# Three edits of a two-layer encoder trunk: last norm's sum, index transposes, last heads of mixer one

## The chip, the cores and the metric

The kernel runs on one core of a Trainium2 chip. The metric is device time in microseconds (us) of one execution, lower is better, as the median of three runs. Beside the timed runs one execution was profiled; its trace is what the rows below are read from. PE is TensorE (matrix multiplies, which write to PSUM), PEld its weight loads, DVE VectorE, ACT ScalarE, POOL GpSimd, SP the engine whose queue issues the loads and stores.

## What is computed

The reference runs 512 tokens of width 1024 through two layers and a last norm, in float32. Cut to what matters here:

```
h = x
layer 0: h = h + even_mixer(rms_norm(h));  h = h + ffn(rms_norm(h))
layer 1: h = h + odd_mixer(rms_norm(h));   h = h + ffn(rms_norm(h))
out = rms_norm(h)            # h * rsqrt(mean(h*h) + 1e-6) * gain

even_mixer, heads A: score[t,s] = sum over 4 index heads of w[t,h] * relu(q_idx[t,h] . k_idx[s])
                     each token keeps its 128 best keys, then softmax attention on those
            heads B: softmax attention with a bias by distance
```

Each mixer half has eight heads; they are worked off in four pairs.

## The kernel before, in words

The residual `h` is held with channels on the partitions: eight blocks of 128 channels by 512 tokens. Each product is made of three matmuls on operands that are split into a high and a low part (`mm3`, lines 179 to 181). Weights come in tiles of 512 KB through SP's queue in the fixed order of a plan and are split by ACT (line 140) and DVE (line 141). A helper `hilo` (lines 186 and 187) splits activations the same way.

The program is written as generators that give out matmuls one unit at a time, so that work on DVE, ACT and POOL lies beside them. `Later` (lines 157 to 172) holds functions that come due after a count of ticks; a tick is given when a token tile of a projection is complete or a channel block is. The order in which an engine gets its instructions isn't the order of the text: when the program is built, a planner puts each engine's instructions in an order by priority (text order) and by when it reckons their inputs to be ready, and after that every engine works strictly in that order. `keep_in_program_order` pins an instruction behind everything already written for its engine.

**The index branch** (lines 641 to 710). Four token tiles of 128 tokens are projected; `evac_idx` norms and rotates one into a tile `qr`, and pushes `turn`, which transposes three 128x128 pieces of it on PE (line 662), splits them with `hilo`, and so fills `iq` and `ik`. All four were pushed with a count of 2. Then the value projection of heads B runs in four pieces (lines 713 to 721): the first completes token tile 0, the second tile 1, the third tile 2, the fourth tile 3, each with a tick. After the second, third and fourth piece the index scores of block 1, 2 and 3 are computed (`idx_scores`, matmuls on line 690); block i needs token tiles 0 to i. Each is followed by its top-k on DVE (`topk`, 16 rounds of two instructions), which runs a round at a time beside later work. `qr` has two buffers, so the third token tile's `qr` can be written only after the first one's transposes.

**The attention pairs** (class `Pair`). `weave(prev, cur, ...)` mixes the transposes and value products of one pair with the scores and softmax of the next. For head e of a pair `soft` adds the bias and takes the minimum on DVE (line 479), the exponential and its sum on ACT (line 481); `norm` takes the reciprocal of four sums on DVE (line 486, pinned) and multiplies four tiles on POOL (line 489); `turn` transposes on PE (line 499); `av` multiplies with the values (lines 516 and 517); `store` ends the head. `norm(0)` stood after the next transposes of the pair before, `norm(1)` at the very end of a `weave`, behind the `store` of the pair before.

**The last norm** (lines 883 to 910). The squares of the first seven channel blocks are summed into `hold_ss` on POOL as the blocks of the last feed-forward product come. The eighth block is computed in two halves of 256 tokens. In the middle of each half `lead_sums` (line 888) adds up `hold_ss` over the partitions: a matmul per token tile with the squares stationary and one column of ones moving, so the sum of a token lands on the partition of that token. When a half is done, `finish` squares the new block on ACT (line 900), adds its sums the same way (line 902), takes root and reciprocal over two columns (lines 197 and 198), and calls `roots` (lines 245 to 254): a diagonal matrix of the roots on DVE (line 248) and a matmul with ones (line 251) bring each token's root to all partitions. Four products (line 909) and four stores (line 910) end the half. fp32 matmuls of this kind are shown as two records each.

Of the kernel before, what the change touches and what calls it, by code (L numbers as in the profile page):

```python
# [10 lines left out]
F32 = mybir.dt.float32  # L11
F32R = mybir.dt.float32r
AF = mybir.ActivationFunctionType
# [4 lines left out]
SEQ = 512  # L18
NT = SEQ // 128
# [67 lines left out]
def trunk(ctx, tc, a, out):  # L87
    nc = tc.nc
# [115 lines left out]
    hold_ss = {}  # L204
# [226 lines left out]
    class Pair:  # L431
# [42 lines left out]
        def soft(self, e, rows):  # L474
            at = {1: 3, 2: 0, 0: 1, 3: 2}
            nms, sms = self.nm[e], self.sm[e]
            for i in rows:
                L, nm, sm = self.L[e][i], nms[:, at[i]:at[i] + 1], sms[:, at[i]:at[i] + 1]
                nc.vector.tensor_tensor_reduce(out=L, in0=self.s[e][i], in1=self.job["bias"][e][i], scale=1.0,
                                               scalar=3e38, op0=OP.add, op1=OP.min, accum_out=nm)  # L480
                nc.scalar.activation(L, L, AF.Exp, scale=-1.0, bias=nm, accum_out=sm)

        def norm(self, e):
            at = {1: 3, 2: 0, 0: 1, 3: 2}
            sms = self.sm[e]
            tc.keep_in_program_order(nc.vector.reciprocal(sms, sms))
            for i in (1, 2, 0, 3):
                L = self.L[e][i]
                nc.gpsimd.tensor_scalar(L, L, sms[:, at[i]:at[i] + 1], 1.0, op0=OP.mult, op1=OP.mult)
# [140 lines left out]
    with ExitStack() as st:  # L630
# [10 lines left out]
        def evac_idx(t, o):  # L641
            raw = mp.tile([128, 5, HD], F32, name="ir", tag="Y", bufs=2)
            nc.scalar.activation(raw.rearrange("p a d -> p (a d)"), o[:, 0:320], AF.Copy, scale=rs[:, t:t + 1])
            nc.vector.tensor_scalar(wi[:, t, :], o[:, 320:324], rs[:, t:t + 1], None, op0=OP.mult)
            st6 = smp.tile([128, 6], F32, name="st6", tag="s6")
            mv = smp.tile([128, 2], F32, name="mv", tag="s2")
            nc.vector.bn_stats(st6, raw[:, 4])
            nc.vector.bn_aggr(mv, st6)
            rstd = smp.tile([128, 1], F32, name="rstd", tag="s1")
            inv_root(rstd, mv[:, 1:2])  # L650
            kk = raw[:, 4]
            nc.vector.tensor_scalar(kk, kk, mv[:, 0:1], rstd, op0=OP.subtract, op1=OP.mult)
            nc.vector.tensor_tensor(kk, kk, lng[:, 0], OP.mult)
            nc.vector.tensor_tensor(kk, kk, lng[:, 1], OP.add)
            qr = sp.tile([128, 6, HD], F32, name="scr2", tag="scr2", bufs=2)
            rope(raw, t, 1, qr[:, 0:5], 5, mp.tile([128, 1024], F32, name="P", tag="P", bufs=2))
            nc.gpsimd.tensor_copy(qr[:, 5], qr[:, 4])

            def turn():
                pt = bank("tp", (128, 4, 128))  # L660
                for b in range(3):
                    nc.tensor.transpose(pt[:, b, :], qr[:, 2 * b:2 * b + 2].rearrange("p a d -> p (a d)"), ident)
                ts_ = slice(t * 128, (t + 1) * 128)
                hilo(iq[:, 0, :, ts_], iq[:, 1, :, ts_], pt[:, 0:2])
                hilo(ik[:, 0, 0, ts_], ik[:, 1, 0, ts_], pt[:, 2])
            later.push(2, turn)

        def at(k):
            pass
# [44 lines left out]
        for f in tok_group("vB", 512, evac_v(VB, 8)):  # L714
            run(f)
            vb += 1
            if vb >= 2 and vb < 5:
                if vb == 2:
                    later.drain()
                idx_scores(vb - 1)  # L720
                aside.q.append(topk(vb - 1))

# [68 lines left out]
        for p in range(4):  # L791
            if p == 2:
                later.drain()
            job = dict(qk=qkA[p], pair=pairs[4 + p], V=lambda e, p=p: VA["t"][:, :, 2 * p + e],
                       bias=[[cmask, work[1], work[2], work[3]]] * 2)
            cur = Pair(mp, job, 2)
            weave(pend, cur, fill, FILL_A[p])
            if p == 0:
# [84 lines left out]
    sums = {}  # L883

    def lead_sums(cols):
        pt = sums["t"] = bank("tp", (128, NT))
        for t in range(cols.start // 128, cols.stop // 128):
            nc.tensor.matmul(pt[:, t:t + 1], hold_ss["t"][:, t * 128:(t + 1) * 128], ones[:, 0:1],
                             start=t * 128 == cols.start, stop=False)

    def finish(c, cols):
        if c < KD - 1:
# [1 line left out]
            nc.scalar.activation(H["h"][:, c, :], H["h"][:, c, :], AF.Copy, scale=gT[:, 4, c:c + 1])  # L894
            return
        w = cols.stop - cols.start
        t0, t1 = cols.start // 128, cols.stop // 128
        pt = sums["t"]
        sq = sp.tile([128, SEQ], F32, name="os", tag="os", bufs=1)
        nc.scalar.activation(sq[:, cols], H["h"][:, c, cols], AF.Square, scale=1.0 / 32.0)  # L900
        for t in range(t0, t1):
            nc.tensor.matmul(pt[:, t:t + 1], sq[:, t * 128:(t + 1) * 128], ones[:, 0:1], start=False,
                             stop=t == t1 - 1)
        nc.scalar.activation(H["h"][:, c, cols], H["h"][:, c, cols], AF.Copy, scale=gT[:, 4, c:c + 1])
        inv_root(rs[:, t0:t1], pt[:, t0:t1])
        r = roots(t0, t1, False)[:, :w]
        for c0, c1 in ((0, 1), (1, 3), (3, 5), (5, 8)):
            v = H["h"][:, c0:c1, cols]
            nc.vector.tensor_tensor(v, v, r[:, None, :].to_broadcast([128, c1 - c0, w]), OP.mult)
# [383 lines left out]
```

## Time and profile before

| | us |
|---|---|
| median of three runs (1224.76 to 1226.49) | 1225.92 |
| the profiled execution | 1225.8 |
| its span, first to last instruction | 1223.8 |
| PE busy in the span | 1204.8 |
| DVE busy | 807.2 |
| ACT busy | 590.6 |
| POOL busy | 192.9 |

Times in the trace count from the start of the span. "Idle before" in square brackets is how long the engine had no instruction running before this one, and what ended that. A row of a timeline merges instructions of one kind that follow one another on their engine (x4), so its length can hold gaps. A matmul's length holds its way through the array: matmuls start closer together than they are long.

### The profile page before, as it was taken

Reading aid. Unit: us, or ns where it says so; the run is one execution under the profiler, and the core shown is the slowest. Engines: PE = TensorE matmul, PEld = TensorE weight load, DVE = VectorE, ACT = ScalarE, POOL = GpSimd, SP = SyncE. Lnnn points to the kernel's source line nnn. Section 1 sums busy time; section 2 is a strip of 40 time slices with the busy share of each in tenths; the row PEclk is TensorE's granted clock in tenths of the full one; section 3 lists DMA queues with packets and bytes.
Section 4 is the critical chain, followed back from the end, with each engine's and each line's share of the span. In section 5 each row is a group of like instructions: output and inputs, shape, how many; then the busy total and the mean of one; then the engine's idle time right before and its main releaser. Section 6 shows DMA issues by size and latency. Waiting matters only on the chain.

```text
span 1223.8 us, 15865 instructions
## 1 busy us (share of the span) xinstructions
PE 1204.8 (98%) x5918; PEld 993.6 (81%) x5918; DVE 807.2 (66%) x1424; ACT 590.6 (48%) x1001; POOL 192.9 (16%) x273
## 2 busy tenths in 40 slices
PE   9999999999999999999999999999999999999997
PEld 8788778877888888888888877778888888888886
DVE  7988987868777777743325466887777777762222
ACT  6555565655444444423224577775544444442221
POOL 1365313131000000000111254322000000000000
PEclk9999999999999999999999999999999999999998
DMA  8232223213332332333322311212332232322311
GB/s 270 69 104 70 87 63 121 70 35 121 104 103 88 102 98 92 104 100 99 95 68 81 121 53 37 70 52 70 104 104 88 102 101 89 104 92 98 103 52 69
DMA packets 35517, 111.70 MB, mean 91 GB/s; under 512 B 4209, under 2 KB 6897, under 8 KB 35441
## 3 DMA queue, kind: packets, MB, share of 16 engines
q1 hardware_dynamic: 35296, 110.68, 28.7%
q8 instruction: 46, 0.75, 0.3%
q14 instruction: 31, 0.25, 0.1%
q10 hardware_dynamic: 144, 0.02, 0.0%
HBM read 108.59 MB, written 2.10 MB: 90 GB/s over the span
## 4 chain that ended last, share of the span: by engine, by line
PE 82%; DVE 9%; ACT 3%; issue 3%; POOL 1%; DMA 1%; SPq 0%; DVEq 0%; POOLq 0%; ACTq 0%
PE acc L179 18%; PE acc L180 18%; PE acc L181 18%; PE s L179 8%; PE s L180 8%; PE s L181 8%; DVE wlo L141 2%; PE tp L499 1%; DVE wk L707 1%; PE tp L516 1%; DVE m L706 1%; PE tp L517 1%; PE s L458 1%; DVE PTl L187 1%; DVE xT L233 1%
## 5 line engine op out<-in xcount | busy, mean ns | idle before, releaser
L141 DVE TENSOR_TENSOR wlo<-raw,whi 128x1024 fp32r<-128x1024 f32 (+3 forms) x189 | 231.8, 1228 | 152.1 <-ACT whi L140 149.2
L140 ACT ACTIVATE whi<-raw 128x1024 fp32r<-128x1024 f32 (+3 forms) x197 | 204.7, 1039 | 218.9 <-PE acc L180 150.8
L179 PE MATMUL acc<-xT,whi 128*128 128x512 f32 x480 | 189.7, 395 | 0.2 <-DVE scr L598 0.2
L180 PE MATMUL acc<-xT,whi 128*128 128x512 f32 x480 | 187.0, 390 | 0.5 <-DVE xT L233 0.5
L181 PE MATMUL acc<-xT,wlo 128*128 128x512 f32 x480 | 187.1, 390 | 0.0
L216 POOL TENSOR_TENSOR scr<-scr,os 128x512 f32<-128x512 f32 x24 | 33.7, 1406 | 709.6 <-ACT os L214 709.6
L179 PE MATMUL acc<-act,whi 128*128 128x512 f32 (+1 forms) x374 | 141.1, 377 | 0.0
L180 PE MATMUL acc<-act,whi 128*128 128x512 f32 (+1 forms) x374 | 141.0, 377 | 0.0
L181 PE MATMUL acc<-act,wlo 128*128 128x512 f32 (+1 forms) x374 | 140.8, 376 | 0.0
L179 PE MATMUL s<-xT,whi 128*128 128x512 f32 x352 | 136.9, 389 | 0.0
L181 PE MATMUL s<-xT,wlo 128*128 128x512 f32 x352 | 136.9, 389 | 0.0
L180 PE MATMUL s<-xT,whi 128*128 128x512 f32 x352 | 136.9, 389 | 0.0
L179 PEld LDWEIGHTS acc<-xT,whi 128*128 128x128 f32 x480 | 90.2, 188 | 20.0 <-issue 1.5
L181 PEld LDWEIGHTS acc<-xT,wlo 128*128 128x128 f32 x480 | 90.1, 188 | 19.3 <-DVE wlo L141 0.2
L180 PEld LDWEIGHTS acc<-xT,whi 128*128 128x128 f32 x480 | 90.2, 188 | 18.9 <-DVE xT L233 0.9
L179 PE MATMUL acc<-whi,xT 128*128 128x512 f32 (+2 forms) x208 | 85.3, 411 | 0.4 <-DVE VB L191 0.2
L181 PE MATMUL acc<-whi,xT 128*128 128x512 f32 (+2 forms) x208 | 81.3, 391 | 0.2 <-DVE xT L233 0.2
L180 PE MATMUL acc<-wlo,xT 128*128 128x512 f32 (+2 forms) x208 | 81.5, 392 | 0.0
L186 ACT ACTIVATE act<-scr 128x512 fp32r<-128x512 f32 x44 | 27.7, 631 | 110.2 <-DVE scr L854 110.2
L181 PEld LDWEIGHTS acc<-act,wlo 128*128 128x128 f32 x374 | 70.4, 188 | 13.0
L180 PEld LDWEIGHTS acc<-act,whi 128*128 128x128 f32 x374 | 70.4, 188 | 12.9
L179 PEld LDWEIGHTS acc<-act,whi 128*128 128x128 f32 x374 | 70.4, 188 | 12.8
(246 smaller groups left out, 2168.4 us busy)
## 6 DMA issues: line engine op xcount, KB each, us to landing
raw<-in_w SPq DMA_DIRECT2D x188, 512.0 KB, 3.4
h<-in_x SPq DMA_DIRECT2D x16, 256.0 KB, 5.4
T<-in_relb SPq DMA_DIRECT2D x8, 256.0 KB, 2.6
raw<-in_w_d SPq DMA_DIRECT2D x4, 264.0 KB, 2.8
out_y<-h SPq DMA_DIRECT2D x4, 256.0 KB, 2.2
raw<-in_w_i SPq DMA_DIRECT2D x3, 324.0 KB, 5.1
out_y<-h SPq DMA_DIRECT2D x2, 384.0 KB, 2.4
ropeC<-in_ropeC SPq DMA_DIRECT2D x2, 256.0 KB, 4.4
```

Source lines behind the costliest of these rows:

```text
L140: nc.scalar.activation(hi[:, x], raw[:, x], AF.Copy)
L141: eng.tensor_tensor(lo[:, x], raw[:, x], hi[:, x].bitcast(F32), OP.subtract)
L179: nc.tensor.matmul(o, lh, rh, start=start, stop=False)
L180: nc.tensor.matmul(o, lh, rl, start=False, stop=False)
L181: nc.tensor.matmul(o, ll, rh, start=False, stop=stop)
L186: nc.scalar.activation(dh, src, AF.Copy)
L187: nc.vector.tensor_tensor(dl, src, dh.bitcast(F32), OP.subtract)
L216: eng.tensor_tensor(ss, ss, sq, OP.add)
L233: nc.vector.scalar_tensor_tensor(xT[1][:, c, :], H["h"][:, c, :], g, xT[0][:, c, :].bitcast(F32), op0=OP.mult, op1=OP.subtract)
L458: ins = nc.tensor.matmul(self.s[e][i], qk[r, b, 0, i * 128:w], qk[r, c, 1, 0:w], start=n == 0, stop=n == 2)
L499: nc.tensor.transpose(pt[:, off:off + 128], self.L[e][i][:, j * 128:(j + 1) * 128], ident)
L516: nc.tensor.matmul(o[:, j * 128:512], v, th[:, off:off + w], start=j == 0, stop=False)
```

## The change

It does three things. The last norm's sums are taken by a matmul with the 128x128 square of ones stationary and the squares moving, which puts each token's sum on every partition; root and reciprocal then run over 128x256, into `R`, and `roots` is no longer called there. The index transposes come due two token tiles at a time: tiles 0 and 1 after two ticks, tiles 2 and 3 after three, and the drain before the first scores goes. For the last pair of the first mixer `norm` is called at the end of `soft`, without the pin, and the later calls return at once.

```diff
--- before.py
+++ after.py
@@ -479,11 +479,17 @@
                 nc.vector.tensor_tensor_reduce(out=L, in0=self.s[e][i], in1=self.job["bias"][e][i], scale=1.0,
                                                scalar=3e38, op0=OP.add, op1=OP.min, accum_out=nm)
                 nc.scalar.activation(L, L, AF.Exp, scale=-1.0, bias=nm, accum_out=sm)
-
-        def norm(self, e):
+            if self.job.get("soon") and len(rows) > 1:
+                self.norm(e, False)
+
+        def norm(self, e, later=True):
+            if later and self.job.get("soon"):
+                return
             at = {1: 3, 2: 0, 0: 1, 3: 2}
             sms = self.sm[e]
-            tc.keep_in_program_order(nc.vector.reciprocal(sms, sms))
+            ins = nc.vector.reciprocal(sms, sms)
+            if later:
+                tc.keep_in_program_order(ins)
             for i in (1, 2, 0, 3):
                 L = self.L[e][i]
                 nc.gpsimd.tensor_scalar(L, L, sms[:, at[i]:at[i] + 1], 1.0, op0=OP.mult, op1=OP.mult)
@@ -663,7 +669,7 @@
                 ts_ = slice(t * 128, (t + 1) * 128)
                 hilo(iq[:, 0, :, ts_], iq[:, 1, :, ts_], pt[:, 0:2])
                 hilo(ik[:, 0, 0, ts_], ik[:, 1, 0, ts_], pt[:, 2])
-            later.push(2, turn)
+            later.push(2 + t // 2, turn)
 
         def at(k):
             pass
@@ -715,8 +721,6 @@
             run(f)
             vb += 1
             if vb >= 2 and vb < 5:
-                if vb == 2:
-                    later.drain()
                 idx_scores(vb - 1)
                 aside.q.append(topk(vb - 1))
 
@@ -792,7 +796,7 @@
             if p == 2:
                 later.drain()
             job = dict(qk=qkA[p], pair=pairs[4 + p], V=lambda e, p=p: VA["t"][:, :, 2 * p + e],
-                       bias=[[cmask, work[1], work[2], work[3]]] * 2)
+                       bias=[[cmask, work[1], work[2], work[3]]] * 2, soon=p == 3)
             cur = Pair(mp, job, 2)
             weave(pend, cur, fill, FILL_A[p])
             if p == 0:
@@ -883,10 +887,9 @@
     sums = {}
 
     def lead_sums(cols):
-        pt = sums["t"] = bank("tp", (128, NT))
-        for t in range(cols.start // 128, cols.stop // 128):
-            nc.tensor.matmul(pt[:, t:t + 1], hold_ss["t"][:, t * 128:(t + 1) * 128], ones[:, 0:1],
-                             start=t * 128 == cols.start, stop=False)
+        w = cols.stop - cols.start
+        sums["t"] = bank("tp")[:, :w]
+        nc.tensor.matmul(sums["t"], ones, hold_ss["t"][:, cols], start=True, stop=False)
 
     def finish(c, cols):
         if c < KD - 1:
@@ -894,16 +897,12 @@
             nc.scalar.activation(H["h"][:, c, :], H["h"][:, c, :], AF.Copy, scale=gT[:, 4, c:c + 1])
             return
         w = cols.stop - cols.start
-        t0, t1 = cols.start // 128, cols.stop // 128
-        pt = sums["t"]
-        sq = sp.tile([128, SEQ], F32, name="os", tag="os", bufs=1)
-        nc.scalar.activation(sq[:, cols], H["h"][:, c, cols], AF.Square, scale=1.0 / 32.0)
-        for t in range(t0, t1):
-            nc.tensor.matmul(pt[:, t:t + 1], sq[:, t * 128:(t + 1) * 128], ones[:, 0:1], start=False,
-                             stop=t == t1 - 1)
+        sq = sp.tile([128, SEQ], F32, name="os", tag="os", bufs=1)[:, :w]
+        nc.scalar.activation(sq, H["h"][:, c, cols], AF.Square, scale=1.0 / 32.0)
+        nc.tensor.matmul(sums["t"], ones, sq, start=False, stop=True)
         nc.scalar.activation(H["h"][:, c, cols], H["h"][:, c, cols], AF.Copy, scale=gT[:, 4, c:c + 1])
-        inv_root(rs[:, t0:t1], pt[:, t0:t1])
-        r = roots(t0, t1, False)[:, :w]
+        r = R[:, cols]
+        inv_root(r, sums["t"])
         for c0, c1 in ((0, 1), (1, 3), (3, 5), (5, 8)):
             v = H["h"][:, c0:c1, cols]
             nc.vector.tensor_tensor(v, v, r[:, None, :].to_broadcast([128, c1 - c0, w]), OP.mult)
```

## Rows read from the trace of the kernel before

**Rows 1.** The page, parts 1 and 4: TensorE's busy time, and the chain by engine.

```profile
PE 1204.8 (98%) x5918; PEld 993.6 (81%) x5918; DVE 807.2 (66%) x1424; ACT 590.6 (48%) x1001; POOL 192.9 (16%) x273
...
PE 82%; DVE 9%; ACT 3%; issue 3%; POOL 1%; DMA 1%; SPq 0%; DVEq 0%; POOLq 0%; ACTq 0%
```

**Rows 2.** Timeline, all engines, after the last matmul; columns: start us, us, instruction, idle before.

```profile
1214.41 0.42 DVE L384 TENSOR_TENSOR h<-acc,h 128x256 f32<-128x256 f32 x1 [2.15 <-PE acc L181]
...
1215.34 0.60 PE L902 MATMUL tp<-ones,os 128*128 128x1 f32 x4 [0.96 <-ACT os L900]
...
1217.03 0.87 PE L251 MATMUL tp<-os,ones 128*128 128x256 f32 x2 [1.08 <-DVE os L248]
...
1217.94 2.48 DVE L909 TENSOR_TENSOR h<-h,tp 128x256 f32<-128x256 f32 x4 [0.96 <-PE tp L251]
```

**Rows 3.** Timeline, PE, the first half's broadcast between the second half's matmuls.

```profile
1209.15 0.59 PE L251 MATMUL tp<-os,ones 128*128 128x256 f32 x2
```

**Rows 4.** Busy time by stretches of 4 us; granted clock (PEclk) third from the end.

```profile
1212.00:1216.00 4.00, 2.98 (x24) 2.69 (x23) 0.69 (x2) 0.94 (x3) 0.00 (x0) 1.00 0.59 208
...
1216.00:1220.00 4.00, 0.87 (x2) 0.30 (x2) 2.65 (x6) 0.25 (x1) 0.00 (x0) 0.68 0.12 42
```

**Rows 5.** Groups by line and shape, ACT; after the bar: busy us, mean ns.

```profile
L1007 ACT ACTIVATE G<-s,nF 128x256 f32<-128x256 f32 x8 | 3.7, 477 | 0.1
```

**Rows 6.** The same view, DVE.

```profile
L384 DVE TENSOR_TENSOR h<-acc,h 128x256 f32<-128x256 f32 x2 | 0.8, 425 | 9.8 <-PE acc L181 9.8
...
L198 DVE RECIPROCAL rs<-rs 128x4 f32<-128x4 f32 x4 | 0.7, 174 | 1.1 <-ACT rs L197 1.1
...
L198 DVE RECIPROCAL rstd<-rstd 128x1 f32<-128x1 f32 x4 | 0.6, 154 | 0.1
...
L198 DVE RECIPROCAL rs<-rs 128x2 f32<-128x2 f32 x2 | 0.3, 166 | 4.1 <-ACT rs L197 4.1
```

**Rows 7.** Chain of waits, last 29 us: start us, us, what.

```profile
1196.14 0.23 PE acc L180
...
1200.54 0.34 PE tp L888 x4
...
1206.02 0.56 PE tp L902 x4
...
1209.32 0.43 PE tp L251 x2
```

**Rows 8.** Timeline around the index transposes: PE, POOL, DVE.

```profile
34.03 0.82 PE L662 MATMUL tp<-ident,scr 128*128 128x128 f32 x6
...
38.40 0.85 PE L662 MATMUL tp<-ident,scr 128*128 128x128 f32 x6 [0.73 <-POOL scr L657]
...
39.18 0.97 PE L690 MATMUL s<-qk 64*128 64x256 f32 x12
...
38.10 0.23 POOL L657 COPY scr<-scr 128x64 f32<-128x64 f32 x1
...
37.20 1.38 DVE L187 TENSOR_TENSOR qk<-tp,qk 128x256 fp32r<-128x256 f32 x4
```

**Rows 9.** Timeline around the last heads of the first mixer: ACT, POOL, PE.

```profile
243.73 0.19 ACT L481 ACTIVATION_READ_ACCUMULATOR P<-P,nm 128x1 f32 x1
...
246.08 2.06 POOL L489 TENSOR_SCALAR P<-P,sm 128x256 f32<-128x256 f32 x4 [12.35 <-DVE sm L486]
...
250.20 2.07 POOL L489 TENSOR_SCALAR P<-P,sm 128x256 f32<-128x256 f32 x4 [2.06 <-DVE sm L486]
...
247.53 1.32 PE L499 MATMUL tp<-ident,P 128*128 128x128 f32 x8 [0.76 <-POOL P L489]
...
281.71 0.50 PE L180 MATMUL acc<-xT,whi 128*128 128x512 f32 x1 [0.47 <-DVE xT L233]
```

**Rows 10.** Timeline, PE, two earlier waits of the first mixer.

```profile
144.86 0.66 PE L499 MATMUL tp<-ident,P 128*128 128x128 f32 x4 [1.59 <-DVE nm L479]
...
170.35 0.39 PE L458 MATMUL tp<-qk 64*128 64x256 f32 x1 [1.31 <-DVE PTl L187]
```

## The prediction

> **What bounds the kernel now.** I read the page first: TensorE is busy for 98% of the span, and the chain that ended last runs for 82% of its length through TensorE's matmuls [rows 1]. So an edit can change the time in three ways only: it adds or removes matmul time, it opens or closes a stretch in which TensorE waits, or it changes the tail behind the last matmul. The second reading was therefore the timeline of the tail; the third was TensorE's own timeline around the index transposes and around the last heads of the first mixer, with what ended its waits. The stages between these places, the two feed-forward blocks above all, are not edited.
>
> The profiled execution took 1225.8 us, 0.1 below the median of the three runs (1225.92); its span is 1223.8, so 2.0 lie around the span. The sum below is made against 1225.8.
>
> **Part 1, the final sum: the tail.** What followed the last matmul is in [rows 2]: the column sums (L902, starting at 1215.34), a root and a reciprocal over two columns, the diagonal (L248), its broadcast by a matmul with ones (L251, 0.87), and at 1217.94 the first product (L909). From L902's start to L909's that is 2.60 us. The new path has three steps: a matmul with the square of ones stationary and 256 columns moving, which leaves the sum on every partition; a root over 128x256; a reciprocal over 128x256. The diagonal and its broadcast go.
>
> - The matmul. Its form, fp32 with 256 moving columns in two passes, is L251's. That took 0.59 in the first half [rows 3] and 0.87 in the tail, where TensorE had just waited for 1.08 [rows 2] and the granted clock of the 4 us was 0.68, after 1.00 in the 4 us before [rows 4]. The new one stands where L902 stands, in the stretch still at 1.00: 0.59, upper end 0.87.
> - The root. The nearest row is an activation with a bias pointer out of PSUM over 128x256: 0.48 [rows 5]. I take it.
> - The reciprocal. No row has it wide. With 1 element per partition it took a mean of 154 ns, with 2 166, with 4 174 [rows 6]: 20 ns for three further elements, 6.7 each. The other bound is an ordinary two-operand instruction over 128x256, 0.43 us [rows 6]. At 6.7 ns, 255 further elements make 0.15 + 1.71 = 1.86 us. I take that, because rows of the operation itself are nearer than a row of another. Ends: 0.43, and 3.2 by the 12 ns between 1 and 2 elements.
>
> With 0.15 for the hand-overs (three gaps of some 0.05, as between L251's end at 1217.90 and L909's start at 1217.94 [rows 2]): 0.59 + 0.48 + 1.86 + 0.15 = 3.08 in place of 2.60, **+0.48**. With the low end it is 1.65, **-0.95**.
>
> [...]
>
> **Part 1, on TensorE before the tail.** In the first half the sums and the broadcast stand between matmuls: 0.34 for L888, 0.56 for L902, which holds a wait of some 0.15, and 0.43 for L251 [rows 7]: 1.33. They become two matmuls of L251's kind, 0.43 each, with the same wait: 1.01, **-0.32**. In the second half L888's 0.34 becomes 0.43, **+0.09**. The wide reciprocal of the first half costs nothing: it lengthens VectorE's work on that half by less than its own 1.86 us, as the diagonal goes, and VectorE had idled 2.15 before the second half's residual add at 1214.41 [rows 2]. Without that cover it would cost up to 1.86. The first half's stores leave SP's queue up to 1 us earlier or later, long before the last ones are queued behind them. Part 1 together: **+0.25**.
>
> **Part 2, index transposes.** In the old order all four token tiles come due together. TensorE runs the transposes of tiles 0 and 1 at 34.03, then matmuls of the projection, waits 0.73 us on GpSimd's copy for tile 3 (it ends at 38.33), runs the other six, and only then the first index scores [rows 8]. The change puts tiles 2 and 3 one piece of the value projection later; the drain that goes found its queue empty before, and would otherwise undo the move. What is late next is the first scores' own input: VectorE finishes splitting tiles 0 and 1 at 37.20 + 1.38 = 38.58 [rows 8], and those matmuls are over at 38.40 - 0.73 = 37.67. If the scores stay there, they wait 1.0 (0.9 and a hand-over) in place of the 0.73; if more matmuls are put ahead of them, they wait for nothing. Later the scores of block 2 wait for tile 2's split. The splits of the first pair ended 4.55 us after its transposes began, 3.7 after they ended [rows 8]; the 12 matmuls of the last piece can cover 12 x 0.23 = 2.7 of that [rows 7]. The number of transposes, splits and scores is unchanged, and no DMA moves. Ends: -0.73, and +4.0 (rival 3). I take half of the gain, **-0.4**: of the two placements one takes the wait away and the other leaves it.
>
> **Part 3, last heads.** The normalising moves up behind the exponentials. For head 0 of the last pair the sums were complete at 243.73 + 0.19 = 243.92, and GpSimd's four products ran only from 250.20 to 252.27 [rows 9], so some 6 us of lateness go. But TensorE did not wait for them. Its waits near here are 0.76 for the pair before, whose normalising stays where it was (products from 246.08), and 0.47 at 281.71 for VectorE's split of the normed input [rows 9]. Only the second can shrink, if the heads end earlier and VectorE starts its residual work sooner. Against that, GpSimd may now take the last pair's head 0 ahead of the pair before: its four products take 2.07, from about 244.2 to 246.3 if they start as the sums come, which makes the pair before 0.2 late; if they start just ahead of 246.08, it is 2.07 late. Ends -0.47 and +2.07; near the first, as GpSimd idled 12.35 us up to 246.08. I take **-0.1**.
>
> **Sum:** +0.25 - 0.4 - 0.1 = -0.25, so 1225.8 - 0.25 = **1225.5 us**.
>
> **Rivals.**
> 1. *The wide reciprocal is cheap* (0.43). Then part 1 is -0.95 - 0.32 + 0.09 = -1.18 and the sum -1.7: 1224.1 us. For it: an ordinary 128x256 instruction takes that. Against: three further elements took 20 ns, where an ordinary instruction's 425 ns over 256 elements make 5 for three.
> 2. *The waits go as meant.* Both marked waits (-0.73 and -0.47) and part of the first mixer's waits on VectorE, 1.59 at 144.86 and 1.31 at 170.35 [rows 10], whose place hangs on when the index work comes in: with half of those two, 1.45, and the dear reciprocal's +0.25 that is -2.4, with the cheap one -3.8: 1223.4 to 1222.0 us. For it: each of these waits stands in the trace. Against: the edits take no work off VectorE.
> 3. *Slower: the second scores wait behind their own transposes.* If the planner puts the scores of block 2 right behind the transposes of tiles 2 and 3, the 3.7 us stand bare on TensorE, with everything queued behind them. With 1.0 for the first scores in place of 0.73 that is +4.0, and with parts 1 and 3 the sum is +4.2: 1230.0 us. Each matmul between takes 0.23 off: with up to 6 there the kernel is slower by more than can be taken for no change (below), with all 12 of the last piece the sum is +1.4. For it: VectorE runs the first top-k rounds just then. Against: the last piece and the next projection are ready.
> 4. *The heads' part does nothing:* TensorE's order stays, and the sum is -0.15: 1225.6, inside the forecast.
>
> **How the numbers follow.** About 0.2%, 2.45 us, is what a measurement of this kernel can tell from no change; against the median the bounds are 1223.5 and 1228.4. Forecast with rival 4: 0.46, all within. Rival 1: 0.20, within but for 0.04. Rival 2: 0.20, beyond the bound but for 0.02. Rival 3: 0.14, slower but for 0.02, when some of the matmuls cover. Faster 0.22, same 0.66, slower 0.12. The range is 1222.4 to 1228.0. Downward it takes in rival 1 and most of rival 2; upward the reciprocal at its upper end (+1.3) with the pair before late by half its bound (+1.0); it leaves out rival 3 and rival 2's edge.
>
> **What would show it.** Right: a reciprocal over 128x256 near 1.9 us in both halves, no diagonal and no broadcast matmul, the first product 3.1 us after the last column sum begins; the first index scores ahead of the transposes of tiles 2 and 3; the last pair's products on GpSimd near 244, with TensorE's waits there as before. Wrong: a reciprocal under 0.6 or over 2.4, a wait above 1 us at the second index scores, or waits of the first mixer that change outside these places.

## The result, and the profile after

The changed kernel takes 1232.84 us, the median of six runs (1230.63 to 1235.56); the kernel before, beside it, 1225.8 (six runs). The ratio is 1.0062 [1.0052, 1.0072]: **slower**, by 0.5 to 0.7%. Predicted were 1225.5 (1222.4 to 1228.0) and a chance of 0.12 for slower. The profiled execution took 1231.66, its span is 1229.6: 5.8 us more than before. The six runs lie in two groups, 1230.63 to 1231.66 us at a mean granted clock of 0.996 to 0.997 and 1234.02 to 1235.56 at 0.992 to 0.993, and the median lies in the gap between them.

TensorE's busy time is nearly the same, 1205.3 us against 1204.8, with 12 matmul records fewer. The page's parts 1 and 4, to set beside [rows 1]:

```profile
PE 1205.3 (98%) x5906; PEld 993.1 (81%) x5906; DVE 811.1 (66%) x1422; ACT 591.3 (48%) x1001; POOL 194.8 (16%) x273
...
PE 86%; DVE 8%; ACT 3%; issue 1%; POOL 1%; DMA 0%; SPq 0%; DVEq 0%; ACTq 0%; POOLq 0%
```

**The tail** went as predicted. Its timeline (TensorE, ScalarE, VectorE), to set beside [rows 2]:

```profile
1220.71 0.70 PE L902 MATMUL tp<-os,ones 128*128 128x256 f32 x2 [0.96 <-ACT os L901]
1221.45 0.47 ACT L197 ACTIVATE R<-tp,epsc 128x256 f32<-128x256 f32 x1 [0.25 <-PE tp L902]
1221.95 1.75 DVE L198 RECIPROCAL R<-R 128x256 f32<-128x256 f32 x1 [1.75 <-ACT R L197]
1223.74 2.50 DVE L908 TENSOR_TENSOR h<-h,R 128x256 f32<-128x256 f32 x4
```

From the column sum's start to the first product it is 3.03 us (2.60 before), and the wide reciprocal takes 1.75.

**The index scores** did not. TensorE's timeline, to set beside [rows 8]; in square brackets its idle time:

```profile
38.70 1.18 PE L696 MATMUL s<-qk 64*128 64x256 f32 x12 [0.69 <-ACT qk L186]
...
45.88 0.82 PE L668 MATMUL tp<-ident,scr 128*128 128x128 f32 x6
...
49.97 0.62 PE L696 MATMUL s<-qk 64*128 64x384 f32 x4 [0.51 <-ACT qk L186]
...
51.72 0.96 PE L696 MATMUL s<-qk 64*128 64x384 f32 x8 [0.23 <-DVE qk L187]
52.97 1.34 PE L696 MATMUL s<-qk 64*128 64x512 f32 x6 [0.29 <-ACT P L701]
55.47 0.49 PE L696 MATMUL s<-qk 64*128 64x512 f32 x1 [1.15 <-ACT P L701]
56.19 0.96 PE L696 MATMUL s<-qk 64*128 64x512 f32 x5 [0.23 <-ACT P L701]
```

In the kernel before, the second scores (64x384) and the third (64x512) stood apart, with 12 matmuls of a projection between them, and waited for nothing:

```profile
46.24 1.33 PE L690 MATMUL s<-qk 64*128 64x384 f32 x12
...
50.44 1.66 PE L690 MATMUL s<-qk 64*128 64x512 f32 x12
```

Now they stand one behind the other. The five waits from 49.97 on make 2.41 us. And behind them the clock falls. Busy time by stretches, after; PEclk, third from the end, is the granted clock as a share of full speed:

```profile
50.00:57.00 7.00, 5.09 (x27) 2.72 (x27) 6.26 (x11) 4.52 (x9) 2.37 (x1) 1.00 0.58 185
57.00:60.00 3.00, 3.00 (x9) 2.31 (x9) 3.00 (x9) 1.31 (x3) 0.14 (x1) 0.58 0.17 68
60.00:63.00 3.00, 3.00 (x13) 2.41 (x12) 2.86 (x9) 0.00 (x0) 0.14 (x1) 0.85 0.00 0
...
135.00:155.00 20.00, 17.95 (x103) 13.96 (x101) 19.89 (x48) 10.45 (x23) 7.71 (x11) 1.00 0.38 117
```

The same view of the kernel before:

```profile
50.00:57.00 7.00, 7.00 (x37) 5.27 (x36) 6.90 (x15) 4.64 (x8) 2.55 (x2) 1.00 0.38 142
57.00:60.00 3.00, 3.00 (x15) 2.49 (x14) 2.72 (x7) 1.55 (x2) 0.14 (x1) 1.00 0.57 171
...
135.00:155.00 20.00, 17.94 (x94) 13.74 (x93) 18.66 (x44) 9.70 (x23) 6.32 (x8) 0.91 0.26 79
```

At 57 to 60 TensorE is busy all the time in both, with 9 matmuls in place of 15. What the low clock costs is read off the rows: 3 x 0.42 + 3 x 0.15 = 1.7 us. The last line of each has a trap: in its profiled execution the kernel *before* had such a low stretch too, between 144 and 150 us (0.72), worth some 20 x 0.09 = 1.8 (1.5 by the table below), and the changed one did not. So the bare difference of the two spans, 5.8, is some 1.5 us smaller than what the edits cost in it.

**The last heads** did not go as meant either. GpSimd's, VectorE's and TensorE's timeline, beside [rows 9]:

```profile
248.48 5.56 POOL L495 TENSOR_SCALAR P<-P,sm 128x256 f32<-128x256 f32 x8 [10.85 <-PE acc L181]
...
248.23 0.16 DVE L490 RECIPROCAL sm<-sm 128x4 f32<-128x4 f32 x1
...
249.99 0.17 DVE L490 RECIPROCAL sm<-sm 128x4 f32<-128x4 f32 x1
...
251.35 1.23 DVE L141 TENSOR_TENSOR wlo<-raw,whi 128x1024 fp32r<-128x1024 f32 x1 [0.17 <-ACT whi L140]
...
251.40 1.63 POOL L495 TENSOR_SCALAR P<-P,sm 128x384 f32<-128x384 f32 x1
...
253.43 1.32 PE L505 MATMUL tp<-ident,P 128*128 128x128 f32 x8 [2.75 <-POOL P L495]
```

GpSimd's products of two shapes (x count, busy us, mean ns), from 248 to 255 us after:

```profile
L495 POOL TENSOR_SCALAR P<-P,sm 128x384 f32<-128x384 f32 x2 | 2.2, 1104 | 0.0
L495 POOL TENSOR_SCALAR P<-P,sm 128x128 f32<-128x128 f32 x2 | 1.2, 584 | 0.0
```

and from 245 to 253 us before:

```profile
L489 POOL TENSOR_SCALAR P<-P,sm 128x384 f32<-128x384 f32 x2 | 1.2, 590 | 0.0
L489 POOL TENSOR_SCALAR P<-P,sm 128x128 f32<-128x128 f32 x2 | 0.8, 376 | 0.0
```

The reciprocal at 248.23 is the last pair's, the one at 249.99 the pair before's (the older pair, below). GpSimd does both heads in one row of eight products, the last pair's first, and the eight take 5.56 where two fours took 2.06 each. The second of the older pair's four took 1.63 beside VectorE's split of a weight tile, where its shape took 0.59 before. TensorE waits 2.75 us for the second four, where it had waited 0.76.

**Where the time came from, along the kernel.** The table below takes the start of each matmul against that of the same matmul before (found by its place in TensorE's order) and says by how much the lag grew in a stretch (median over 8 us around each mark; marks in us of the kernel before; the last column ends at the end of the span). The versions below are in it.

| version | 25 to 100 (index) | 100 to 155 | 155 to 220 | 220 to 290 (last heads) | 290 to end |
|---|---|---|---|---|---|
| after | +4.79 | -1.54 | +0.28 | +1.87 | +0.05 |
| sum alone | -0.01 | -1.56 | +0.36 | +0.02 | -0.07 |
| sum, index | +4.75 | -0.01 | +0.15 | +0.04 | -0.07 |
| sum, heads | -0.04 | -1.61 | +0.32 | +3.49 | -0.08 |
| last tile alone late | -0.27 | -0.02 | +0.05 | -0.01 | -0.08 |
| one tick earlier | +2.14 | -1.55 | +0.25 | -0.01 | -0.08 |
| whole change, pinned | +6.08 | -0.04 | +0.05 | +3.44 | -0.01 |
| index, filled | +3.23 | -1.53 | +0.43 | +0.05 | +0.02 |
| index, two operands | +4.59 | -1.57 | +0.35 | 0.00 | -0.01 |
| index, scaled on ScalarE | +2.15 | -1.54 | +0.32 | +0.06 | -0.04 |
| both last pairs | -0.02 | -1.55 | +1.83 | -1.57 | -0.12 |
| all four pairs | +0.33 | -1.53 | +0.34 | -1.37 | 0.00 |
| logarithm, exponential | +0.06 | -1.55 | +0.32 | -1.56 | +0.99 |

The -1.55 of the second column is before's own low stretch. Up to the mark at 25 the executions differ by up to 0.5 us either way with no edit in sight. In its profiled execution the change is therefore +4.8 in the index part, +1.9 at the last heads and nothing in the tail.

### The profile page after: what moved, and what is told of

The parts are those of the page before. It is cut to its first block, busy times and chain, and to the rows that moved or that the text cites. A ratio compares the mean times of both kernels' runs of the same rounds, so it can differ in the third digit from the quotient of the medians.

```text
span 1229.6 us, 15829 instructions
## 1 busy us (share of the span) xinstructions
PE 1205.3 (98%) x5906; PEld 993.1 (81%) x5906; DVE 811.1 (66%) x1422; ACT 591.3 (48%) x1001; POOL 194.8 (16%) x273
## 4 chain that ended last, share of the span: by engine, by line
PE 86%; DVE 8%; ACT 3%; issue 1%; POOL 1%; DMA 0%; SPq 0%; DVEq 0%; ACTq 0%; POOLq 0%
PE acc L179 19%; PE acc L180 18%; PE acc L181 18%; PE s L179 8%; PE s L180 8%; PE s L181 8%; PE tp L505 2%; DVE wlo L141 1%; PE tp L522 1%; PE tp L523 1%; PE s L458 1%; DVE PTl L187 1%; DVE wk L713 1%; DVE m L712 1%; DVE scr L379 1%
```

## The experiments

All times are medians; ratios are to the kernel before, run beside each version on the same chip, where it took 1224.76 to 1225.72. The chips are not the same for all versions, so versions are compared by their ratios. "Index undone" restores `push(2, turn)` and the drain, "heads undone" takes `soon` away.

**The three parts.** The final sum with the heads, index undone:

```diff
-            later.push(2 + t // 2, turn)
+            later.push(2, turn)
...
+                if vb == 2:
+                    later.drain()
```

> The changed kernel with the index transposes put back (all four token tiles after two ticks, drain restored); last norm's sum and early last heads kept. Theory A (three separate effects: index transposes cost about 3.9 us, early last heads 2.0, the sum nothing): about 1225.8 + 2.0 = 1227.8 us, TensorE's wait at the pair before the last still about 2.8 us. Rival B (the early heads only look late because everything before them runs late): 1225.8, and that wait is back at about 0.8.

1228.1 us, 1.0027 [1.0016, 1.0037]. The wait behind GpSimd's products is there (2.77).

The final sum with the index, heads undone (`-, soon=p == 3`):

> The changed kernel with the early last heads taken out; index transposes in pairs and the new sum kept. Theory A: about 1225.8 + 3.9 = 1229.7 us, TensorE's wait at the pair before the last back at about 0.8 us, the waits at the second and third index scores (about 3 us together) and the stretch at half clock behind them still there. Rival B (the index part costs nothing by itself): 1225.8.

1230.41 us, 1.0043 [1.003, 1.0056]; the waits of the index scores and the low clock are those of after (0.59 from 57 to 60), the heads' wait is back at 0.75.

The final sum alone, both undone:

> The kernel of before with the new sum alone. Theory A: within 0.5 us of before (1225.3 to 1226.3): tail longer by some 0.4 (2.60 becomes about 3.0), two matmuls fewer in the first half save 0.3. Rival C (the wide reciprocal is a loss to be seen): 1227 or more. Rival D (the new sum gains, and the loss elsewhere hides it): under 1225.

1225.8 us, 1.0005 [0.9996, 1.0014]: no difference that can be told. By ratios the heads add 0.0022 to the sum alone (2.7 us) and the index 0.0038 (4.7 us), and the parts add up: 1.0005 + 0.0022 + 0.0038 = 1.0065, within the interval of the whole change, 1.0062 [1.0052, 1.0072].

**Why the heads cost.** The whole change, with the early reciprocal pinned as the late one is:

```diff
-            ins = nc.vector.reciprocal(sms, sms)
-            if later:
-                tc.keep_in_program_order(ins)
+            tc.keep_in_program_order(nc.vector.reciprocal(sms, sms))
```

> The changed kernel with the early normalising pinned behind VectorE's earlier instructions, as it was before; nothing else undone. Theory P (without the pin the last pair's reciprocal goes ahead of the pair before's, so GpSimd does the last pair's four products first and the pair before is late): GpSimd's order is back, TensorE's wait at the pair before falls from 2.8 to about 0.8 us, and the time from about 1232 to about 1230 us. Rival Q (the early place itself costs, by products on GpSimd beside VectorE's work): the wait and the time stay.

1233.8 us, 1.0073 [1.006, 1.0086]. The pin did not bring the older pair forward: a pin holds an instruction only behind what is already written for its engine, and the last pair's early reciprocal is written before the older pair's late one. GpSimd did the eight products in the order of after, and the wait was 2.76 again, so this run did not test the order. As a repeat of after it shows how much the clock adds: behind the same waits it was lower for longer in this execution (0.88, 0.50 and 0.64 in the stretches from 50, 57 and 60 us, where after has 1.00, 0.58 and 0.85), and it fell behind the heads' wait as well (0.92 from 240 to 260), which makes +6.08 and +3.44 in the table.

Head 1 of the last pair alone at once (index undone; `and e == 1` at both places of `soon`):

> The new sum, old index transposes, early normalising for head 1 of the last pair alone. Theory G: head 0 is what stood in the way on GpSimd, so the wait at the pair before is 0.76 as in the kernel of before, and the time is that of the sum alone within 0.6 us. Rival Q: head 1's early products cost as well, 0.5 us or more above the sum alone.

1225.43 us, 1.0 [0.9991, 1.0009], the wait at 0.75. The price needs head 0 at once, whose products can pass the older pair's.

Both last pairs at once (index undone):

```diff
-                       bias=[[cmask, work[1], work[2], work[3]]] * 2, soon=p == 3)
+                       bias=[[cmask, work[1], work[2], work[3]]] * 2, soon=p >= 2)
```

> The new sum, old index transposes, and early normalising for the last two pairs, not the last alone, so that the pair before is normalised ahead of the last pair again. Theory G (the loss of the early heads is GpSimd's order: the pair before stands behind the last pair): the 2.8 us wait goes, and the old 0.76 goes too, since the pair before now has its products some 10 us before it needs them: about 0.8 us below the kernel with the sum alone. Rival Q (early products cost by themselves, on GpSimd beside VectorE): the wait at that place stays above 0.8 and the time above the kernel with the sum alone.

1223.76 us, 0.9986 [0.9977, 0.9995]: faster than before. GpSimd's timeline has the heads one by one, each four products long:

```profile
235.68 2.06 POOL L495 TENSOR_SCALAR P<-P,sm 128x256 f32<-128x256 f32 x4 [3.66 <-DVE sm L490]
245.13 2.07 POOL L495 TENSOR_SCALAR P<-P,sm 128x256 f32<-128x256 f32 x4 [7.39 <-PE acc L181]
250.86 2.06 POOL L495 TENSOR_SCALAR P<-P,sm 128x256 f32<-128x256 f32 x4 [3.66 <-DVE sm L490]
```

No wait of TensorE for these products is left, and the one at 281.71 [rows 9] is gone too: 0.76 + 0.47 = 1.23 of the table's 1.57. (Its +1.83 from 155 to 220 is a low stretch of the clock: 0.91 from 160 to 180.) What cost time was not normalising at once but doing it for one pair and not for its neighbour. How the 2 us divide between GpSimd's order and VectorE's work beside it is read from the trace alone; no run has one without the other.

All four pairs of this part (`soon=True`):

> All four pairs of the first mixer's second part normalised at once, not the last two alone. Theory A: what cost 2.3 us in the change was GpSimd's order between two neighbouring pairs that are treated differently; here no neighbours of this part differ, the one border lies between the last pair of the part before and the first pair of this one, where a product of GpSimd of the older pair stands behind the newer one's: a TensorE wait of up to 2 us there, 1223.8 to 1226. Theory B: normalising at once is good wherever it stands: 1223.8 or up to 0.5 us below (the waits on POOL's P that before shows in this part are under 1 us each).

1223.45 us, 0.9987 [0.9979, 0.9996]. The older part's border, where the first theory looked for a wait, shows none: no time is lost from 100 to 220, and none of TensorE's waits from 225 to 300 is left.

All pairs of both parts:

> All pairs of both parts of the first mixer normalised at once, so that no border between two kinds of pairs is left. Theory A (GpSimd's order at the border is the price): no border, so no wait of TensorE behind GpSimd's products of about 2 us anywhere, and the time is that of the version with the last two pairs, 1223.8, within 1 us. Theory B (dividing early pulls vector work ahead of what TensorE needs sooner): the more pairs, the later the splits and transposes, and the time rises to 1225 to 1228.

1225.28 us, 1.0 [0.9991, 1.0009]. The last heads gain as much (-1.42 from 220 to 290), and the +2.23 from 155 to 220 is a low stretch of the clock (0.91 from 160 to 180, 20 x 0.09 = 1.8) for all but 0.4, near the +0.3 that most versions show there. The median lies 1.8 us above that of the four pairs alone. From 160 to 180 us TensorE is idle for 1.84 us here (busy 18.16 of 20), and for 1.30 from 155 to 185 with four pairs (busy 28.70 of 30), as the second theory has it; but the version with both last pairs had the same low stretch with 1.30 us of idle time from 160 to 180 (busy 18.70 of 20). The cause was not tried, and the second theory stays open.

**Why the index cost.** Only the last token tile late (heads undone):

```diff
-            later.push(2 + t // 2, turn)
+            later.push(2 + t // 3, turn)
```

> The new sum, no early heads, and only token tile 3 moved one piece later; tiles 0 to 2 come due together as before. Theory C (the pairs cost because the second scores need tile 2's split at once and the 12 matmuls of the last piece are spent on covering it, so that second and third scores stand back to back): now the second scores have their input early, the last piece stands between second and third scores again, the waits of 0.5, 0.2, 0.3, 1.15 and 0.2 us go, the clock stays full, and the 0.73 wait on GpSimd's copy goes as well: at or up to 0.7 us below the sum alone. Rival V (any later transposes cost, as VectorE runs top-k rounds then): 2 us or more above the sum alone, with the wait moved to the third scores.

1225.24 us, 1.0002 [0.9993, 1.001]. No wait is shown at the second and third scores, and they stand apart as before. The third take 2.25 us in place of 1.66, and the wait of 0.73 for GpSimd's copy, which the first theory had gone as well, stays. TensorE's timeline:

```profile
45.66 0.49 PE L668 MATMUL tp<-ident,scr 128*128 128x128 f32 x3
46.09 1.31 PE L696 MATMUL s<-qk 64*128 64x384 f32 x12
...
50.28 2.25 PE L696 MATMUL s<-qk 64*128 64x512 f32 x12
```

All transposes one tick earlier (`1 + t // 2`, heads undone):

> The new sum, no early heads, and the index transposes in pairs but one piece earlier: tiles 0 and 1 after one tick, tiles 2 and 3 after two. Theory C: pairs as such are harmless, being late is what costs: the second scores have their input in time, no wait above 0.5 us at second or third scores, time within 0.7 us of the sum alone, or below. Rival V2 (splitting the transposes into two pairs costs by the order that the planner then makes): 2 us or more above the sum alone.

1227.93 us, 1.0019 [1.001, 1.0028]. The second and third scores are free here too, but the order built around them has small waits at 32 to 38 us (1.2 in all) and a new one, of 1.2, behind GpSimd's work for a pair. Moving the transposes by pairs, earlier or later, had a price of 2 us or more.

The index part with five unused matmuls ahead of each half of the third scores:

```diff
             for hp in range(2):
+                if i == 3:
+                    warm = bank("tp")
+                    for j in range(5):
+                        tc.keep_in_program_order(nc.tensor.matmul(warm, xT[0][:, 0, 0:128], xT[0][:, 0, :],
+                                                                  start=j == 0, stop=j == 4))
                 ss_ = [bank("s")[:, :w] for _ in range(2)]
```

> The index part alone with the final sum, as in the run of these two parts, and ten more fp32r matmuls of 512 columns ahead of the third index scores, five before each half, whose result nobody reads (work that is added and not used); TensorE's order of everything else is that run's. Theory A: about 2 us of what the index part costs are not its waits (0.5, 0.2, 0.3 and 1.15 us) but the half clock afterwards (granted clock 0.59 and 0.84 from 57 to 63 us, some ten matmuls at 0.43 us in place of 0.23). Then the added matmuls (2.3 us, of which 1.4 us lie in the waits of 0.29 and 1.15) keep the granted clock at 1.00 from 57 to 63 us, and the time comes out below the 1230.4 us of the run without them, at 1228.5 to 1229.7. Theory B: only the waits cost. Then the time is that run's or up to 1 us above it, 1230.4 to 1231.4, whatever the clock row shows.

1228.01 us, 1.0027 [1.0016, 1.0039]: with ten matmuls more, 2.4 us below the run without them by the medians (2.0 by the ratios), a little under the range of the first theory. The intervals of the two runs overlap, so the reading rests on the traces: +3.23 in the table in place of +4.75. TensorE's busy time by stretches:

```profile
50.00:57.00 7.00, 6.77 (x36) 4.12 (x35) 6.23 (x10) 4.54 (x9) 2.54 (x2) 1.00 0.53 180
57.00:60.00 3.00, 3.00 (x14) 2.45 (x13) 2.86 (x8) 1.18 (x2) 0.00 (x0) 1.00 0.04 16
```

The last third scores end where they ended (the next matmul of the projection starts at 56.69, 56.83 without the additions), and what is saved lies behind them: the clock stays at 1.00. So the waits were paid twice, once as idle time and once as a low clock behind.

The longest wait, 1.15, ends on ScalarE's relu, which needs its buffer back from VectorE's first multiplication. In after, that relu, the multiplication and GpSimd's split beside it are (timelines of ScalarE, VectorE and GpSimd):

```profile
54.92 0.49 ACT L701 ACTIVATE P<-s 128x384 f32<-128x384 f32 x1 [1.62 <-DVE wk L703]
...
52.95 1.88 DVE L703 TENSOR_SCALAR wk<-P,wi 128x384 f32<-128x384 f32 x1 [0.43 <-ACT P L701]
...
52.25 2.37 POOL L141 TENSOR_TENSOR wlo<-raw,whi 128x1024 fp32r<-128x1024 f32 x1 [3.98 <-ACT whi L140]
```

In the version with the last tile late the same shape, with no split beside it, took 0.40:

```profile
49.20 0.40 DVE L703 TENSOR_SCALAR wk<-P,wi 128x384 f32<-128x384 f32 x1
```

The one of 1.88 us ends at 54.83, 0.21 after the split (54.62). Two runs ask whether that is the cause. The multiplication in a form with two tensor operands, the second unused:

```diff
-                        nc.vector.tensor_scalar(wk, rl, wi[:, i, 0:1], 0.0, op0=OP.mult, op1=OP.add)
+                        nc.vector.scalar_tensor_tensor(wk, rl, wi[:, i, 0:1], rl, op0=OP.mult, op1=OP.bypass)
```

> The index part with the final sum, and the first multiplication of the index weights (a TENSOR_SCALAR on VectorE, which took 1.88 us for 128x384 while GpSimd's split ran, 0.35 to 0.47 elsewhere) written as a SCALAR_TENSOR_TENSOR with two tensor operands, whose second operand is not used; TensorE's and GpSimd's orders are the same. Theory A: the wait of 1.15 us in the third index scores is that stretched multiplication: in its new form it takes about 0.6 us as the others of line 705 do, the wait shrinks to 0.1 or less, less idle time stands before 57 us, and the time falls from 1230.4 to 1228 or 1229.3 (to 1227 if the granted clock stays at 1.00). Theory B: the scores wait because two of them stand back to back on too few banks, whatever the multiplication takes: the new form is as slow beside the split, or the wait stays at 0.9 or more, and the time is 1229.9 to 1231.

1229.19 us, 1.0031 [1.0019, 1.0042]; the interval overlaps that of the version it was made from. It did not tell the theories apart, since the new form was held up as well:

```profile
52.62 1.69 DVE L703 SCALAR_TENSOR_TENSOR wk<-P,wi 128x384 f32<-128x384 f32 x1 [0.43 <-ACT P L701]
...
51.52 2.37 POOL L141 TENSOR_TENSOR wlo<-raw,whi 128x1024 fp32r<-128x1024 f32 x1 [3.59 <-ACT whi L140]
```

It ended at 54.31, 0.42 after the split. The wait stayed at 0.96 and the clock fell (0.50 from 57 to 60). So the multiplication went to ScalarE:

```diff
-                        nc.vector.tensor_scalar(wk, rl, wi[:, i, 0:1], 0.0, op0=OP.mult, op1=OP.add)
+                        nc.scalar.activation(wk, rl, AF.Copy, scale=wi[:, i, 0:1])
```

> The index part with the final sum, and the first multiplication of the index weights on ScalarE (an ACTIVATE with a scale) in place of VectorE; TensorE's order differs by one matmul of a projection that stands ahead of the second and third index scores, not behind them, GpSimd's not at all. Theory A: the wait of 0.96 to 1.15 us in the third index scores was VectorE's multiplication, stretched to 1.69 to 1.88 us beside GpSimd's split; on ScalarE it takes 0.5 us (the relu before it takes 0.49) and the wait falls below 0.4; TensorE's busy time from 50 to 57 us rises by 0.5 or more, and the time against before falls from 1.0043 to 1.0020 to 1.0035. Theory B: the scores wait because two stand back to back on too few banks: ScalarE's multiplications stand between the relus that free the banks, the waits sum up to 2 us as before, and the ratio stays at 1.0035 to 1.0055.

1227.93 us, 1.0024 [1.0015, 1.0033], against 1.0043 [1.003, 1.0056] with the multiplication on VectorE; the ends of the intervals just overlap. TensorE's order differs by one matmul of a projection. Its timeline and its busy time by stretches:

```profile
52.52 2.13 PE L696 MATMUL s<-qk 64*128 64x512 f32 x8 [0.29 <-ACT P L701]
54.82 0.96 PE L696 MATMUL s<-qk 64*128 64x512 f32 x4 [0.17 <-ACT P L701]
```

```profile
50.00:57.00 7.00, 6.16 (x30) 3.54 (x30) 5.40 (x12) 5.85 (x11) 2.52 (x2) 1.00 0.52 183
57.00:60.00 3.00, 3.00 (x15) 2.47 (x14) 2.86 (x8) 0.60 (x1) 0.14 (x1) 1.00 0.00 0
```

The 1.15 is gone, the clock stays up, and the index part costs 2.15 in place of 4.75 (by the traces). The first theory holds: VectorE held up behind GpSimd's split made the longest wait, and with it went the low clock. What is left is the scores standing back to back (waits of 1.09 in all).

**The tail.** Both last pairs at once, with a logarithm and an exponential for the root and the reciprocal:

```diff
-        inv_root(r, sums["t"])
+        nc.scalar.activation(r, sums["t"], AF.Ln, bias=epsc)
+        nc.scalar.activation(r, r, AF.Exp, scale=-0.5)
```

> The version with both last pairs normalised at once, and in the last stage the root and the wide reciprocal (0.47 and 1.75 us in the tail of the changed kernel) replaced by two ACTIVATEs on ScalarE, a logarithm and an exponential of minus half of it. Theory A: the wide reciprocal is the largest piece between the last sum and the last products, and two ACTIVATEs of 0.47 us each give back 0.47 + 1.75 - 0.94 = 1.28 us per half where it ends the time, so 1222.5 against 1223.8 (1222.0 to 1223.2). Theory B: the two functions make ScalarE load a table before each (1.28 us for a load in the trace), which falls between the sum and the products: 1223.8 - 1.3 + 1.3 to 2.6, so 1223.8 to 1225.1.

1224.91 us, 0.9997 [0.9988, 1.0006]: the second theory. ScalarE's timeline in the tail:

```profile
1212.58 1.28 ACT L907 ACT_TABLE_LOAD   x1
1213.87 0.47 ACT L907 ACTIVATE R<-tp,epsc 128x256 f32<-128x256 f32 x1
1214.36 1.28 ACT L908 ACT_TABLE_LOAD   x1
1215.66 0.42 ACT L908 ACTIVATE R<-R 128x256 f32<-128x256 f32 x1
```

Two loads stand in the path, and the table's last column has the price, +0.99, where the version it was made from has -0.12. The root form has none in the second half's tail.

**The parts that were right, together.** All four pairs at once, and the last tile late:

> The final sum by the square of ones, all four pairs of the second part normalised at once, and the transposes of the last token tile alone put off behind the second index scores. Theory A: the two edits touch different stretches (around 40 us, and 180 to 280 us) and add up: 1223.45 less the 0.5 us by which putting off the last tile alone stood below the final sum alone, 1222.9 (1222.4 to 1223.4). Theory B: the delayed transposes move VectorE's work of all later pieces by a little, so that pairs and pieces meet differently: 1223.5 to 1225.5.

1223.99 us, 0.9987 [0.9978, 0.9995]; its own before took 1225.72. The ratio is that of the four pairs alone, so the late tile adds nothing that can be told. These versions are 0.13% faster than before: real by their intervals, and under the 0.2% that the prediction named.

## Why the prediction was wrong

The prediction failed in two of its three parts: part 2 had -0.4 and measured +4.8, part 3 had -0.1 and measured +1.9.

**Part 1 was right.** The matmul, the root and the reciprocal were 0.59, 0.48 and 1.86 predicted and 0.70, 0.47 and 1.75 measured. The step from one element to four [rows 6] gave the price of 256 to within 0.11 us, and rival 1, the cheap reciprocal, is out. Measured from one element (0.15) to 256 (1.75), the step is (1.75 - 0.15) / 255 = 6.3 ns per element, where the rows had given 6.7. Part 1's sum, +0.25, came out as no difference in any version.

**Part 2 failed, at the step "what is late next".** It named the first scores and the second, and there it stopped. The first were to wait 1.0 or nothing; they stayed where they were and waited 0.69 in place of 0.73, so the gain of 0.4 did not come. For the second it reckoned that the last piece's 12 matmuls can cover 2.7 us; they did, and 0.51 and 0.23 were left. But those matmuls were what had stood *between* the second scores and the third. Spent ahead of the second, they leave the third right behind them, waiting for ScalarE to read the second's sums, and the prediction has no line for that. Taken apart, as an estimate from the rows: idle time 2.41 - 0.04 for the first scores; five waits whose row begins at the modelled end of a matmul, 0.39 after its start, while the next could have started 0.23 after it, so 0.16 more each, 0.8; the low clock, 1.7. Together 4.9, against 4.79 in the table. The same reckoning gives 4.6 for the form with two operands (2.21 - 0.08 + 0.8 + 1.7), against 4.59.

Rival 3 had the side and the order of size (+4.0), but not the mechanism: it wanted the second scores bare behind their own transposes, and by its own count the case that came, "all 12", was +1.4. Neither GpSimd's split beside VectorE nor the clock stood anywhere in the sum, though [rows 4] showed a granted clock of 0.68 in a stretch with waits.

**Part 3 failed at the choice between its ends, and at the length of the products.** The event was foreseen, GpSimd taking the last pair's head 0 ahead of the pair before, with an end of +0.2 if the products start as the sums come. They did start so: at 248.48, which is 244.57 on the clock of before (the lag there is 3.91), 0.4 behind the estimate. But the sum took the four at their undisturbed 2.07, and in the new place VectorE works beside them. The older pair's four began at 250.95, where 246.08 + 3.91 = 249.99 had been due: 0.96 late, of which some 0.2 was in the sum, some 0.4 is the later start, and 0.43 a product of 128x128 that took 0.80 in place of 0.37. Then their second product took 1.63 in place of 0.59, 1.04 more. Together 2.0. That this is the size of the other end (+2.07) is chance: that end had the products start just ahead of the older pair's. That GpSimd had idled 12.35 us was no reason to stay near the low end: idle time before an engine's work says nothing of what runs beside that work. The waits went from 0.76 and 0.47 to 2.75 and 0.32: +1.84, against +1.87 in the table. In the run of sum and heads a low stretch came behind that wait (0.83 from 245 to 255, the table's +3.49), and in the pinned one too (+3.44).

**Rivals 2 and 4** did not come. The waits that rival 2 counted on at the last heads go only when both neighbours are treated alike.

## What to carry to other kernels

When independent work is put in front of a late consumer, ask what that work used to separate: the cover is moved, not made. When one of two neighbours in a pipeline gets its step earlier, look on every shared engine for the older one's work that it can pass, and for what the neighbouring engine does at the new place; treat both alike or neither. And price a cluster of short waits on a TensorE-bound kernel with the clock behind it: here 2.4 us of idle time cost 4.8.

## What the runs showed of the hardware

- **The clock after short waits.** In all four profiled executions with index waits of 2.2 to 2.4 us in all between 49 and 57 us, the granted clock fell behind them, to a mean of 0.50 to 0.59 from 57 to 60 us (in the pinned version it fell beside the last scores already, 0.88 from 50 to 57); with two operands, at 0.50, matmuls of 128x512 start 0.43 us apart there, in before, at 1.00, 0.23. In the one with 1.1 us, and in the one with the waits of the third scores filled (0.76 left), it stayed at 1.00. Behind the one wait of 2.75 to 2.77 us at the last heads it fell in two executions of three (0.83 from 245 to 255 with sum and heads, 0.92 from 240 to 260 in the pinned version; in after 1.00 from 245 to 260). At 135 to 155 us TensorE is busy 17.9 of 20 us in the kernels before and after, and the clock falls there in some executions and not in others: it did before (0.91) and with sum and index (0.91), it did not in after (1.00). Such a stretch is worth about 1.6 us.
- **VectorE beside GpSimd.** A multiplication of 128x384 took 1.88 us in place of 0.40, and in the form with two tensor operands 1.69 in place of 0.62, and ended 0.2 to 0.4 us after GpSimd's split. Both forms were held up to about the split's end; by what means one engine holds up the other, no trace shows. It goes the other way round too: where VectorE's split began first (251.35), GpSimd's product of 128x384 took 1.63, to 0.45 after the split's end. Being held up costs only what waits behind it: with the last tile late, one of 128x512 took 1.57 beside a split (0.47 in after with none), and no wait of TensorE followed.
